# Five norms of an encoder in a different order, a softmax multiply moved to DVE, a last norm read from its bank

## The chip, the core and the metric

The kernel runs on one core of a Trainium2 chip. The metric is device time in microseconds (us), the median of several runs. The core's engines are named as in the profile: PE multiplies matrices, DVE and ACT work along rows of 128 partitions, POOL is the third of that kind, and SP issues transfers. Each engine works through its own queue in order and waits at semaphores for what other engines or transfers have to finish first.

## The reference, cut

Two requests of 512 and 256 tokens go through the same two layers, one of each kind, with a model width of 1024. The kernel lays them side by side as 768 columns.

```python
def rmsnorm(x, g, eps=NORM_EPS):
    return x * lax.rsqrt(jnp.mean(x * x, axis=-1, keepdims=True) + eps) * g

for layer in range(DEPTH):                       # 2
    if layer % 2 == 0:
        h = rmsnorm(x, ln_mix_e[j])
        qa, ka, va, qb, kb, vb = jnp.split(h @ w_in_e[j], EVEN_SPLITS, axis=-1)
        a_out = neighbourhood_attention(qa, ka, va, rpb[j])
        qb, kb = rope(rmsnorm(qb, q_norm_b[j])), rope(rmsnorm(kb, k_norm_b[j]))
        b_out = gqa_attention(qb, kb, vb)        # 8 query heads on 2 key heads, softmax
        x = x + jnp.concatenate([a_out, b_out], axis=-1) @ w_out_e[j]
    else:
        h = rmsnorm(x, ln_mix_o[j])
        qc, kc, vc = jnp.split(h @ w_in_o[j], ODD_SPLITS, axis=-1)
        o = rmsnorm(diff_attention(rope(qc), rope(kc), vc, lam), subln_g[j]) * (1.0 - lam_init)
        x = x + o.reshape(B, T, DIFF_WIDTH) @ w_out_o[j]
    h = rmsnorm(x, ln_mlp[layer])
    x = x + jnp.square(jax.nn.relu(h @ w_up[layer])) @ w_down[layer]
return rmsnorm(x, ln_f)
```

## The kernel before

**Layout.** Everything is kept feature by token: x is eight tiles of 128 features by 768 tokens, six token tiles of 128 (TT). Each 32-bit operand of a projection is split into a high part, made by a copy (whi, xh), and a low part, the remainder (wlo, xl), and a product is three matmuls: high by high, high by low, low by high. Functions wsplit (L76) and split (L108) make the parts; the high one is ACT's (or DVE's for every other weight piece at the start), the low one DVE's.

**A norm (class Norm, L127).** The rows of x carry the gain only; the factor 1/rms of each token is applied behind the projection. add (L140) squares a feature tile on ACT and adds it to acc on DVE. rstd (L154) sums acc over the features by tiny matmuls into ss (L161), scales it to ms on DVE (L164) and raises it to the power -1/2 on POOL, rt (L166), one column for each token tile. Where a factor along the columns is needed, spread (L169) makes it by matmuls into the bank pb (L178) and DVE copies that to R (L180). PSUM has eight banks in two groups, three named mm and five named at; a tile waits until the readers of an earlier tile in its bank are done.

**Stages in order.** even_attention (L303) loads x and the first weights, splits them in a loop over eight feature tiles (L320) with the squares of the tile before in each turn, projects keys and values of the six token tiles (proj_kv, tile kvp; kv_out scales them by rt and hands the keys to norm_rope) and then the queries (proj_q, tile qp). Its tables function calls rstd and builds the rotary tables. Attention units and further projections alternate. A unit of the query heads takes two heads: scores gs, their maximum m (DVE, L495), ge = exp (ACT, L497), reciprocal ri (DVE, L500), and the division of both heads' ge, one on DVE (L501), one on POOL (L502); six units for each pair of heads, 24 in all, of 512 keys or of 256. Then ge is transposed on PE (gpt_ps, L443) and multiplied by the values. The odd layer projects values first (proj_v, tile dvp, ACT's dv behind it) and then queries and keys (dqk). Each MLP is a product in seven partial products (up, L856, and dn, L1022) on sums c of quarters of x (t and c at L792 to L817); finish (L869) multiplies the result z by R. The last norm (final, L1065) runs in two halves of 384 tokens: squares, rstd, spread, and eight multiplies by gain and R (L1093), each followed by its transfer out, alternately on SP's and on ACT's queue.

**What sets the order.** A scheduler places the instructions of each engine's queue by the order in which the code is written, by priorities (tc.high_priority() raises them) and by estimated readiness. On the chip each queue is fixed.

Of the kernel before, what the change touches and what calls it, by code (L numbers as in the profile page):

```python
# [37 lines left out]
def kernel(ctx: ExitStack, tc: tile.TileContext, a: dict, y: bass.AP):  # L38
# [22 lines left out]
    def ps_tile(tag, name):  # L61
        return psum.tile([P, 512], F32, tag=tag, name=name, bufs=BANKS[tag])
# [66 lines left out]
    def gcol(g, k):  # L129
        return gains[:, g, k : k + 1]  # L130

    class Norm:
# [22 lines left out]
        def rstd(self, s0=0):  # L155

            n = len(self.tiles)
            ss = ps_tile("at", "ss")
            for i, t in enumerate(self.tiles):
                for j, part in enumerate(self.parts):  # L160
                    nc.tensor.matmul(ss[:, 2 * i : 2 * i + 2], part[:, t * P - s0 : (t + 1) * P - s0], ones,  # L161
                                     start=j == 0, stop=j == len(self.parts) - 1)
            ms = spool.tile([P, TT], F32, tag="ms", name="ms", bufs=2)[:, :n]
            nc.vector.tensor_scalar(ms, ss[:, 0 : 2 * n : 2], 1.0 / D, 1e-6, op0=ALU.mult, op1=ALU.add)  # L164
            rt = cpool.tile([P, TT], F32, tag="rt", name="rt", bufs=2)[:, :n]
            nc.gpsimd.tensor_tensor(out=rt, in0=ms, in1=nhalf[:, :n], op=ALU.pow)  # L166
            return rt

        def spread(self, rt, R=None):  # L169

            if R is None:
                R = cpool.tile([P, NT], F32, tag="R", name="R", bufs=1)
            for c in range(0, len(self.tiles), 4):
                ts_ = self.tiles[c : c + 4]
                s, e = ts_[0] * P, ts_[-1] * P + P
                pb = ps_tile("at", "pb")
                for i, t in enumerate(ts_):
                    nc.tensor.matmul(pb[:, i * P : (i + 1) * P], rt[:, c + i : c + i + 1].broadcast_to([P, P]), ident,  # L178
                                     start=True, stop=True)
                nc.vector.tensor_copy(R[:, s:e], pb[:, : e - s])  # L180
            return R


    def proj_tok(col, xs, t, ps):
# [116 lines left out]
    def even_attention():  # L301
# [18 lines left out]
        for k in range(KD):  # L320
            c = slice((k % 4) * 256, (k % 4) * 256 + 256)
            wsplit(w0[k // 4][0][:, c], w0[k // 4][1][:, c], raws[k // 4][:, c], k % 2 == 0)
            xs.append(split(x0s[k], "x", gcol(G_E, k)))
            if k:
                nm.add(x0s[k - 1])
        nm.add(x0s[KD - 1])
        col0 = wcol(w0)

        ropeE = xo_tile("ropeE").rearrange("p (a t d) -> p a t d", a=2, d=HD)
# [64 lines left out]
        def proj_kv():  # L394
            col = col0
            kT.append(qk("gk"))

            gv.append(ap.tile([P, 9, P], F32R, tag="v", name="gv", bufs=3)[:, :8, :].rearrange("p (t a) (b d) -> p t (a b) d", a=2, b=2))
            gv.append(ap.tile([P, 2, 4, HD], F32R, tag="gvp", name="gvp", bufs=1))
            pend = []  # L400
            for t in range(TT):
                ps = ps_tile("mm" if t < 3 else "at", "kvp")
                yield from proj_tok(col, xs, t, ps)
                pend.append((t, ps))
                if t == 3:
                    tables()
                while pend and t >= 3:
                    kv_out(*pend.pop(0))

        def kv_out(t, ps):  # L410
            r = rts[0][:, t : t + 1]
            v = gv[t // 4][:, t % 4]
            pv = ps[:, P:256].rearrange("p (h d) -> p h d", d=HD)
            nc.scalar.activation(v[:, 0:4:3], pv, AF.Copy, scale=r)
            nc.vector.scalar_tensor_tensor(out=v[:, 1:3], in0=pv, scalar=r, in1=v[:, 0:4:3].bitcast(F32),
                                           op0=ALU.mult, op1=ALU.subtract)
            norm_rope(ps[:, :P], 2, t, tabs[1], kT)

        def proj_q(s):
            col = wgroup("w_in_e")  # L420
            for j in range(2):
                gq[2 * s + j] = qk(f"gq{2 * s + j}")
            for t in range(TT):
                ps = ps_tile("mm", "qp")
                yield from proj_tok(col, xs, t, ps)
                norm_rope(ps[:, :256], 4, t, tabs[0], [gq[2 * s], gq[2 * s + 1]])

# [48 lines left out]
        def gqa_unit(j, t):  # L476
            if t == 0:
                o[j] = xo_tile("go")
            if t % 2 == 0:
                vals.append(Values(j, t))  # L480
                del vals[:-2]
            now = vals[-1]
            prev = vals[-2] if len(vals) > 1 else None
            q, k = gq[j], kT[0]
            tk = slice(t * P, (t + 1) * P)
            k0, nk = (0, 4) if t < 4 else (TS, 2)
            ks = slice(k0, k0 + nk * P)
            l2 = spool.tile([P, 2], F32, tag="l2", name="l2")

            def f_s():  # L490
                ss = scores("gs", nk * P, lambda i, hp, s: q[hp, i, s], lambda i, hp, s: k[hp, i, s], tk, ks)
                es_ = []
                for h, s in enumerate(ss):
                    m = spool.tile([P, 1], F32, tag="m", name="m")
                    nc.vector.tensor_reduce(out=m, in_=s, axis=AX.X, op=ALU.max, negate=True)  # L495
                    e = ap.tile([P, 512], F32, tag="e", name="ge", bufs=6)[:, : nk * P]
                    nc.scalar.activation(e, s, AF.Exp, bias=m, scale=1.0, accum_out=l2[:, h : h + 1])  # L497
                    es_.append(e)
                ri = spool.tile([P, 2], F32, tag="ri", name="ri")
                nc.vector.reciprocal(ri, l2)  # L500
                nc.vector.tensor_scalar(es_[0], es_[0], ri[:, 0:1], None, op0=ALU.mult)  # L501
                nc.gpsimd.tensor_tensor(out=es_[1], in0=es_[1], in1=ri[:, 1:2].broadcast_to([P, nk * P]), op=ALU.mult)  # L502
                now.es.append(es_)

            def f_t():
                v = now if t % 2 else prev
                if v:
                    v.turn()

            def f_v():  # L510
                v = now if t % 2 else prev
                if v:
                    v.values()

            return f_s, f_t, f_v, lambda: None


# [98 lines left out]
    def odd_attention(xs, nm, sg, spill):  # L616
# [17 lines left out]
        def proj_v(n):  # L634
            col = wgroup("w_in_o")
            v = vs[n] = ap.tile([P, TT, 256], F32, tag="v", name=f"dv{n}", bufs=2)
            pend = []
            for t in range(TT):
                ps = ps_tile("mm" if n or t < 3 else "at", "dvp")
                yield from proj_tok(col, xs, t, ps)  # L640
                pend.append((t, ps))
                if not rts and t == TT - 1:
                    rts.append(nm.rstd())
                while rts and pend:
                    t_, ps = pend.pop(0)
                    nc.scalar.activation(v[:, t_, :], ps[:, :256], AF.Copy, scale=rts[0][:, t_ : t_ + 1])  # L646
# [419 lines left out]
    def final(x, sq, s):  # L1066

        acc = cpool.tile([P, NT], F32, tag="acc", name="acc", bufs=1) if s else accs[0]
        R = cpool.tile([P, NT], F32, tag="R", name="R", bufs=1) if s else accs[1]
        accs[:] = [acc, R]  # L1070
        ms = (0, 2, 4, 6, 1, 3, 5, 7) if s else (1, 3, 5, 7, 0, 2, 4, 6)
        sl = slice(s, s + HT)
        nm = Norm(None, (s, s + HT), acc)
        rt = []

        def part(i):
            if i == 0:
                nc.scalar.activation(acc[:, sl], x[ms[0]][:, sl], AF.Square)
                nm.parts = [acc[:, sl]]
                for n, m in enumerate(ms[1:]):  # L1080
                    t = sq()
                    nc.scalar.activation(t, x[m][:, sl], AF.Square)
                    if n < 5:
                        nc.vector.tensor_tensor(out=acc[:, sl], in0=acc[:, sl], in1=t, op=ALU.add)
                    else:
                        nm.parts.append(t)
            elif i == 1:
                rt.append(nm.rstd(s))
            else:
                nm.spread(rt[0], R)  # L1090
                for k in ms:
                    yt = x[k][:, sl]
                    nc.vector.scalar_tensor_tensor(out=yt, in0=yt, scalar=gcol(G_F, k), in1=R[:, sl], op0=ALU.mult, op1=ALU.mult)  # L1093
                    (nc.sync, nc.scalar)[k // 2 % 2].dma_start(y[:, k, sl], yt)

        return part
# [146 lines left out]
```

## Time and profile before

| | us |
|---|---|
| median of three runs | 1766.36 (1765.38 to 1767.30) |
| the profiled execution, its own time | 1770.48 |
| its span in the trace | 1768.2 |
| PE busy | 1721.2 (97%) |
| DVE busy | 1396.3 (79%) |
| ACT busy | 825.0 (47%) |
| POOL busy | 593.0 (34%) |

The span runs from the first to the last recorded instruction; the rest of the execution's own time lies around it. The mean granted clock of PE over the span is 0.987 of full speed. A line of the waits says which tile an engine waited for, who released it, and for how long. A line of the timeline has the start, the length, the engine, the line of the kernel, and the tile with its sources; behind it in brackets the idle time of the engine before it and what ended that. [...]

### The profile page before, as it was taken

The page shows a single profiled execution, that of the slowest core. Times are in us where ns is not written, and L with a number is a line of the kernel's source. Part 1 is how long each engine was busy: PE and PEld are TensorE (multiplying, and loading weights), DVE is VectorE, ACT ScalarE, POOL GpSimd, SP SyncE. Part 2 cuts the span into 40 slices and gives each one's busy share as a digit, 9 for nine tenths or more (in the row PEclk, how much of TensorE's full clock was granted, in tenths as well). Part 3 has the DMA queues.
Part 4 walks back from the last instruction along what each step waited for, and adds up shares of the span by engine and source line. Part 5 has one row for each costly group of instructions (what it writes and reads, how often), then busy time and mean ns, then how long its engine had stood idle before and what let it go on. Part 6 is the DMA issues. An engine that isn't in the chain of part 4 may idle for free.

```text
span 1768.2 us, 28354 instructions
## 1 busy us (share of the span) xinstructions
PE 1721.2 (97%) x10994; PEld 1635.5 (92%) x10994; DVE 1396.3 (79%) x2182; ACT 825.0 (47%) x1509; POOL 593.0 (34%) x456
## 2 busy tenths in 40 slices
PE   7999999999999999999999999999989999999997
PEld 7887888899999999999999999988989999999997
DVE  7777746588899878799656767776898888797995
ACT  6675544354333354444425555554543333544441
POOL 1421000023555505475021212220236556054750
PEclk8999999999999999999999999999999999999998
DMA  4111223312554497764211101112124544977621
GB/s 167 49 34 37 69 67 101 125 55 99 166 165 166 165 342 280 285 199 158 97 48 49 45 29 46 51 55 94 57 99 165 166 157 162 338 290 268 220 90 72
DMA packets 74597, 235.42 MB, mean 133 GB/s; under 512 B 7904, under 2 KB 25056, under 8 KB 74464
## 3 DMA queue, kind: packets, MB, share of 16 engines
q1 hardware_dynamic: 52480, 186.93, 31.7%
q0 software_dynamic: 7168, 25.17, 3.8%
q10 hardware_dynamic: 14816, 21.52, 3.4%
q8 instruction: 86, 1.41, 0.3%
q14 instruction: 47, 0.39, 0.1%
HBM read 182.47 MB, written 50.33 MB: 132 GB/s over the span
## 4 chain that ended last, share of the span: by engine, by line
PE 67%; DVE 18%; issue 7%; ACT 4%; POOL 2%; DMA 1%; DVEq 0%; POOLq 0%; SPq 0%; ACTq 0%
PE dn L1022 25%; PE dqk L190 8%; PE up L856 6%; PE opa L202 5%; PE dvp L190 4%; DVE z L875 3%; DVE wlo L81 3%; DVE z L864 3%; PE opb L202 3%; PE npa L202 2%; DVE t L864 2%; PE ds L268 2%; PE dpv L716 2%; ACT z L877 2%; DVE t L792 2%
## 5 line engine op out<-in xcount | busy, mean ns | idle before, releaser
L856 PE MATMUL up<-c,whi 128*128 128x384 f32 x1824 | 469.8, 339 | 0.0
L1022 PE MATMUL dn<-th,whi 128*128 128x384 f32 x1792 | 460.8, 338 | 0.0
L856 PEld LDWEIGHTS up<-c,whi 128*128 128x128 f32 x1824 | 332.6, 189 | 0.1
L1022 PEld LDWEIGHTS dn<-th,whi 128*128 128x128 f32 x1792 | 325.7, 188 | 0.7 <-DVE th L117 0.5
L856 PE MATMUL up<-c,wlo 128*128 128x384 f32 x912 | 310.1, 340 | 3.8 <-DVE wlo L81 3.6
L1022 PE MATMUL dn<-th,wlo 128*128 128x384 f32 x896 | 302.9, 338 | 0.5 <-DVE wlo L81 0.5
L986 POOL TENSOR_TENSOR ch<-ch,wd 128x1024 f32<-128x1024 f32 x60 | 187.6, 3136 | 117.7 <-DVE wlo L81 94.5
L841 POOL TENSOR_TENSOR s<-wraw 128x512 f32<-128x512 f32 x56 | 105.8, 1907 | 331.6 <-DMA wraw<-in_w_up_dram 308.0
L81 DVE TENSOR_TENSOR wlo<-ch,whi 128x1024 fp32r<-128x1024 f32 x88 | 166.9, 1912 | 27.7 <-ACT whi L80 27.4
L856 PEld LDWEIGHTS up<-c,wlo 128*128 128x128 f32 x912 | 172.3, 189 | 8.5 <-DVE wlo L81 8.3
L80 ACT ACTIVATE whi<-ch 128x1024 fp32r<-128x1024 f32 x88 | 93.2, 1064 | 176.6 <-PE dn L1022 138.8
L1022 PEld LDWEIGHTS dn<-th,wlo 128*128 128x128 f32 x896 | 168.2, 188 | 1.1 <-DVE wlo L81 1.1
L117 DVE TENSOR_TENSOR th<-tr,th 128x1536 fp32r<-128x1536 f32 x56 | 142.8, 2553 | 12.8 <-ACT th L116 12.7
L81 DVE TENSOR_TENSOR wlo<-wraw,whi 128x1024 fp32r<-128x1024 f32 (+3 forms) x132 | 136.3, 1034 | 17.5 <-ACT whi L80 17.0
L80 ACT ACTIVATE whi<-wraw 128x1024 fp32r<-128x1024 f32 (+3 forms) x128 | 116.8, 914 | 68.0 <-PE opb L202 24.6
L190 PE MATMUL dqk<-whi,xh 128*128 128x256 f32 x384 | 116.1, 302 | 2.2 <-ACT dv L646 2.2
L877 ACT ACTIVATE z<-z 128x1536 f32<-128x1536 f32 x32 | 47.7, 1489 | 140.5 <-DVE z L875 139.5
L190 PE MATMUL dqk<-whi,xl 128*128 128x256 f32 x384 | 108.6, 283 | 0.0
L190 PE MATMUL dqk<-wlo,xh 128*128 128x256 f32 x384 | 108.4, 282 | 0.0
L701 ACT ACTIVATE de<-ds,m 128x512 f32<-128x512 f32 (+1 forms) x96 | 58.4, 613 | 81.7 <-DVE m L699 81.7
L116 ACT ACTIVATE th<-tr 128x1536 fp32r<-128x1536 f32 x56 | 82.8, 1478 | 24.4 <-DMA tr<-T 15.6
L864 DVE TENSOR_TENSOR z<-up,z 128x384 f32<-128x384 f32 x168 | 89.8, 548 | 4.5 <-PE up L856 4.4
(217 smaller groups left out, 3772.6 us busy)
## 6 DMA issues: line engine op xcount, KB each, us to landing
wd<-in_w_down_dram SPq DMA_DIRECT2D x84, 512.0 KB, 4.9
tr<-T SPq DMA_DIRECT2D x56, 768.0 KB, 5.3
wraw<-in_w_up_dram SPq DMA_DIRECT2D x64, 512.0 KB, 3.7
T<-t POOLq DMA_DIRECT2D x64, 384.0 KB, 3.0
T<-z ACTq DMA_DIRECT2D x32, 576.0 KB, 3.0
ch<-in_w_down_dram SPq DMA_DIRECT2D x28, 512.0 KB, 7.4
wraw<-in_w_in_o_dram SPq DMA_DIRECT2D x24, 512.0 KB, 3.7
wraw<-in_w_in_e_dram SPq DMA_DIRECT2D x16, 512.0 KB, 3.8
```

What stands on the lines that cost most here:

```text
L80: nc.scalar.activation(hi, raw, AF.Copy)
L81: nc.vector.tensor_tensor(out=lo, in0=raw, in1=hi.bitcast(F32), op=ALU.subtract)
L116: nc.scalar.activation(hi, src, AF.Copy)
L117: nc.vector.tensor_tensor(out=lo, in0=src, in1=hi.bitcast(F32), op=ALU.subtract)
L190: nc.tensor.matmul(ps[:, :256], st[:, tk], col(k, part, 0, 256), start=(k == 0 and i == 0), stop=(k == KD - 1 and i == 2))
L202: nc.tensor.matmul(ps[:, : e - s], w, mv[:, s:e], start=(k == 0 and i == 0), stop=(k == nk - 1 and i == 2))
L841: nc.gpsimd.tensor_tensor(out=d_, in0=x_, in1=y_, op=ALU.add)
L856: nc.tensor.matmul(ps, part[a_][:, base + k * P : base + (k + 1) * P], t[:, b_], start=start and k + i == 0, stop=stop and k == 3 and i == 2)
L864: nc.vector.tensor_tensor(out=out, in0=x_, in1=y_, op=op)
L877: nc.scalar.activation(z, z, AF.Square)
L986: nc.gpsimd.tensor_tensor(out=t, in0=t, in1=new.pop((i, rp)), op=ALU.add)
L1022: nc.tensor.matmul(ps, w[a_][:, c : c + P], th[:, b_, q], start=i + q + a_ + b_ == 0, stop=i == NG - 1 and q == ND - 1 and a_ == 1)
```

## The change

It has six parts.

1. In rstd, ms and rt are placed at high priority, in every norm.
2. In the first norm, the squares come behind all eight splits, and rstd and all uses of rt come behind the sixth token tile of keys and values instead of the fourth. The first query tile takes its bank from the at group.
3. In the odd layer rstd is called behind the fourth value tile instead of the sixth.
4. In the query heads' softmax the second head's ge is divided by DVE as well.
5. spread is cut in two; bcast makes the bank pb alone. In the last norm the multiplies of DVE read R from that bank and not from a copy.
6. In the second half of the last norm (s = 0), three feature tiles are multiplied by the gain beforehand on ACT, R is copied from the bank by ACT, and POOL multiplies these three by R; DVE has the other five. One more tile of squares is added to acc there, so ss has two parts instead of three.

```diff
@@ rstd
-            nc.vector.tensor_scalar(ms, ss[:, 0 : 2 * n : 2], 1.0 / D, 1e-6, op0=ALU.mult, op1=ALU.add)
             rt = cpool.tile([P, TT], F32, tag="rt", name="rt", bufs=2)[:, :n]
-            nc.gpsimd.tensor_tensor(out=rt, in0=ms, in1=nhalf[:, :n], op=ALU.pow)
+            with tc.high_priority():
+                nc.vector.tensor_scalar(ms, ss[:, 0 : 2 * n : 2], 1.0 / D, 1e-6, op0=ALU.mult, op1=ALU.add)
+                nc.gpsimd.tensor_tensor(out=rt, in0=ms, in1=nhalf[:, :n], op=ALU.pow)
@@ even_attention, splits
-            if k:
-                nm.add(x0s[k - 1])
-        nm.add(x0s[KD - 1])
+        for x0 in x0s:
+            nm.add(x0)
@@ proj_kv
-                if t == 3:
+                if t == TT - 1:
                     tables()
-                while pend and t >= 3:
-                    kv_out(*pend.pop(0))
+                    while pend:
+                        kv_out(*pend.pop(0))
@@ proj_q
-                ps = ps_tile("mm", "qp")
+                ps = ps_tile("mm" if s + t else "at", "qp")
@@ gqa_unit
                 nc.vector.tensor_scalar(es_[0], es_[0], ri[:, 0:1], None, op0=ALU.mult)
-                nc.gpsimd.tensor_tensor(out=es_[1], in0=es_[1], in1=ri[:, 1:2].broadcast_to([P, nk * P]), op=ALU.mult)
+                nc.vector.tensor_scalar(es_[1], es_[1], ri[:, 1:2], None, op0=ALU.mult)
@@ odd layer, proj_v
-                if not rts and t == TT - 1:
+                if not rts and t == 3:
                     rts.append(nm.rstd())
@@ final
-                    if n < 5:
+                    if n < (5 if s else 6):
...
+                if not s:
+                    for k in ms[:3]:
+                        nc.scalar.activation(x[k][:, sl], x[k][:, sl], AF.Copy, scale=gcol(G_F, k))
...
-                nm.spread(rt[0], R)
+                early = () if s else ms[:3]
+                pb = nm.bcast(rt[0])
+                if early:
+                    nc.scalar.activation(R[:, sl], pb, AF.Copy)
                 for k in ms:
                     yt = x[k][:, sl]
-                    nc.vector.scalar_tensor_tensor(out=yt, in0=yt, scalar=gcol(G_F, k), in1=R[:, sl], op0=ALU.mult, op1=ALU.mult)
+                    if k in early:
+                        nc.gpsimd.tensor_tensor(out=yt, in0=yt, in1=R[:, sl], op=ALU.mult)
+                    else:
+                        nc.vector.scalar_tensor_tensor(out=yt, in0=yt, scalar=gcol(G_F, k), in1=pb, op0=ALU.mult, op1=ALU.mult)
```

Line numbers behind the first part move by up to 15. Three places of the instruction order follow.

**PE at the start**, around the sums of the first norm (ss); kvp are the keys and values, qp the queries. Before:

```order
L190 MATMUL kvp<-whi,xh 128x256
L190 MATMUL kvp<-wlo,xh 128x256
L190 MATMUL kvp<-whi,xl 128x256 x4
L161 MATMUL ss<-ones,acc 128x2 x6
L190 MATMUL kvp<-whi,xh 128x256
```

Now:

```order
L196 MATMUL kvp<-whi,xh 128x256
L196 MATMUL kvp<-wlo,xh 128x256
L196 MATMUL kvp<-whi,xl 128x256
L161 MATMUL ss<-ones,acc 128x2 x6
L196 MATMUL qp<-whi,xh 128x256
L196 MATMUL qp<-wlo,xh 128x256
```

Before, 96 kvp matmuls stand ahead of ss and 48 behind it; now all 144 stand ahead, and two query tiles of 24 matmuls each follow.

**DVE at the first MLP's norm**; t and c are the sums of quarters of x, wlo a weight's low part. Before:

```order
L792 SCALAR_TENSOR_TENSOR t<-x_4166,gains,t 128x384 x3
L117 TENSOR_TENSOR c_4752<-t,c_4752 128x384
L81 TENSOR_TENSOR wlo<-wraw,whi 128x512
L117 TENSOR_TENSOR c_4756<-t,c_4756 128x384
L117 TENSOR_TENSOR c_4760<-t,c_4760 128x384
L117 TENSOR_TENSOR c_4763<-t,c_4763 128x384
L792 SCALAR_TENSOR_TENSOR t<-x_4250,gains,t 128x384
L164 TENSOR_SCALAR ms<-ss 128x6
L792 SCALAR_TENSOR_TENSOR t<-x_4319,gains,t 128x384 x3
L117 TENSOR_TENSOR c_4770<-t,c_4770 128x384
```

Now:

```order
L797 SCALAR_TENSOR_TENSOR t<-x_4082,gains,t 128x384
L797 SCALAR_TENSOR_TENSOR t<-x_4166,gains,t 128x384 x3
L166 TENSOR_SCALAR ms<-ss 128x6
L81 TENSOR_TENSOR wlo<-wraw,whi 128x512
L117 TENSOR_TENSOR c_4752<-t,c_4752 128x384
L117 TENSOR_TENSOR c_4756<-t,c_4756 128x384
L117 TENSOR_TENSOR c_4760<-t,c_4760 128x384
L117 TENSOR_TENSOR c_4763<-t,c_4763 128x384
L797 SCALAR_TENSOR_TENSOR t<-x_4250,gains,t 128x384
L797 SCALAR_TENSOR_TENSOR t<-x_4319,gains,t 128x384 x3
```

ms, with POOL's rt behind it, stands ahead of one wlo, the four c and one t that it stood behind.

**PE in the odd layer's value projection**, around ss. Before:

```order
L190 MATMUL dvp_8984<-wlo_8855,xh_8784 128x256
L190 MATMUL dvp_8984<-whi_8854,xl_8785 128x256
L161 MATMUL ss_9009<-ones_77,acc_8764 128x2 x6
L190 MATMUL dqk_9040<-whi_9028,xh_8791 128x256
L190 MATMUL dqk_9040<-wlo_9029,xh_8791 128x256
L190 MATMUL dqk_9040<-whi_9028,xl_8792 128x256
```

Now:

```order
L196 MATMUL dvp_8934<-wlo_8855,xh_8784 128x256
L196 MATMUL dvp_8934<-whi_8854,xl_8785 128x256
L161 MATMUL ss_8959<-ones_77,acc_8764 128x2 x6
L196 MATMUL dvp_8974<-whi_8848,xh_8791 128x256
L196 MATMUL dvp_8974<-wlo_8849,xh_8791 128x256
L196 MATMUL dvp_8974<-whi_8848,xl_8792 128x256
```

ss has moved ahead of the last two value tiles; before, the first query and key tile dqk followed it at once.

## Rows read from the trace of the kernel before

**Rows 1.** Waits of PE: tile and line, releaser, us in total, times, longest
```profile
PE pb L178 <- POOL rt L166: 9.9, 3, 5.0
...
PE kvp L190 <- ACT xh L119: 5.5, 1, 5.5
...
PE gpt_ps L443 <- DVE ge L501: 4.2, 4, 2.2
...
PE dqk L190 <- ACT dv L646: 2.2, 1, 2.2
```

**Rows 2.** Windows: us, busy (count) of PE, PEld, DVE, ACT, POOL; clock, DMA
```profile
22.00:45.00 23.00, 19.12 (x117) 18.34 (x117) 16.48 (x60) 10.03 (x32) 7.98 (x13) 0.78 0.24 68
65.00:193.00 128.00, 120.07 (x838) 101.17 (x838) 100.82 (x213) 80.23 (x217) 30.49 (x35) 0.99 0.11 32
415.00:420.00 5.00, 5.00 (x21) 5.00 (x20) 4.78 (x7) 1.24 (x2) 0.00 (x0) 0.50 0.00 0
535.00:640.00 105.00, 102.73 (x577) 99.86 (x576) 95.14 (x109) 41.95 (x44) 49.43 (x35) 1.00 0.60 206
```

**Rows 3.** Timeline of the start: begin, length, row, [idle before it, releaser]
```profile
20.21 1.01 DVE L120 SCALAR_TENSOR_TENSOR xl<-x,gains,xh 128x768 fp32r<-128x768 f32 x1
...
21.14 0.95 DVE L152 TENSOR_TENSOR acc<-acc,sq 128x768 f32<-128x768 f32 x1
...
23.48 2.17 PE L161 MATMUL ss<-ones,acc 128*128 128x2 f32 x12 [1.46 <-DVE acc L152]
...
26.01 1.51 POOL L166 TENSOR_TENSOR rt<-ms,nhalf 128x6 f32<-128x6 f32 x1 [24.69 <-DVE ms L164]
...
27.56 1.14 ACT L414 ACTIVATE gv<-kvp,rt 128x128 fp32r<-128x128 f32 x4 [6.87 <-POOL rt L166]
```

**Rows 4.** Timeline of the first query-head softmaxes, DVE and POOL
```profile
65.38 0.48 DVE L501 TENSOR_SCALAR ge<-ge,ri 128x512 f32<-128x512 f32 x1
...
69.57 1.04 POOL L502 TENSOR_TENSOR ge<-ge,ri 128x512 f32<-128x512 f32 x1 [2.48 <-DVE ss L354]
...
69.67 1.22 DVE L501 TENSOR_SCALAR ge<-ge,ri 128x512 f32<-128x512 f32 x1
```

**Rows 5.** Groups by line and shape, DVE: busy us, mean ns, idle before
```profile
L501 DVE TENSOR_SCALAR ge<-ge,ri 128x512 f32<-128x512 f32 x16 | 14.3, 893 | 0.6
```

**Rows 6.** Timeline of the first MLP's norm, DVE, POOL and PE
```profile
406.80 2.31 DVE L792 SCALAR_TENSOR_TENSOR t<-x,gains,t 128x384 f32<-128x384 f32 x4
...
412.27 1.69 POOL L166 TENSOR_TENSOR rt<-ms,nhalf 128x6 f32<-128x6 f32 x1 [8.22 <-DVE ms L164]
...
414.02 2.93 PE L178 MATMUL pb<-ident,rt 128*128 128x128 f32 x12 [3.76 <-POOL rt L166]
...
422.50 0.96 DVE L864 TENSOR_TENSOR t<-z 128x768 f32<-128x768 f32 x1 [1.00 <-ACT z L877]
...
426.86 0.56 DVE L864 TENSOR_TENSOR z<-up,z 128x384 f32<-128x384 f32 x1 [2.21 <-PE up L856]
```

**Rows 7.** Timeline of the second MLP's norm, PE
```profile
1301.38 2.93 PE L178 MATMUL pb<-ident,rt 128*128 128x128 f32 x12 [4.96 <-POOL rt L166]
```

**Rows 8.** Timeline of the odd layer's norm, PE and POOL
```profile
881.66 0.28 PE L190 MATMUL dvp<-whi,xl 128*128 128x256 f32 x1
...
881.78 1.40 PE L161 MATMUL ss<-ones,acc 128*128 128x2 f32 x12
...
883.46 1.34 POOL L166 TENSOR_TENSOR rt<-ms,nhalf 128x6 f32<-128x6 f32 x1 [60.07 <-DVE ms L164]
...
885.75 0.42 PE L190 MATMUL dqk<-wlo,xh 128*128 128x256 f32 x1
...
885.96 0.41 PE L190 MATMUL dqk<-whi,xl 128*128 128x256 f32 x1
```

**Rows 9.** Timeline of the last norm's second half, DVE
```profile
1754.59 0.55 DVE L864 TENSOR_TENSOR x<-x,dn 128x384 f32<-128x384 f32 x1 [0.93 <-PE dn L1022]
...
1760.94 4.32 DVE L1093 SCALAR_TENSOR_TENSOR x<-x,gains,R 128x384 f32<-128x384 f32 x8
```

More of the change, by code (lines that the diff above doesn't have):

```diff
@@ L173, in spread, with bcast @@
             for c in range(0, len(self.tiles), 4):
[L174 to L180, printed above, removed]
-            return R
+                pb = self.bcast(rt, c)
+                s = self.tiles[c] * P
+                nc.vector.tensor_copy(R[:, s : s + pb.shape[1]], pb)
+            return R
+        def bcast(self, rt, c=0):
+            ts_ = self.tiles[c : c + 4]
+            pb = ps_tile("at", "pb")
+            for i in range(len(ts_)):
+                nc.tensor.matmul(pb[:, i * P : (i + 1) * P], rt[:, c + i : c + i + 1].broadcast_to([P, P]), ident,
+                                 start=True, stop=True)
+            return pb[:, : len(ts_) * P]
     def proj_tok(col, xs, t, ps):
```

## The prediction

> **What bounds the kernel now.** I read the page's busy times first: PE is busy for 97% of the span, DVE for 79%. Little can come from shorter work on the other engines; only PE's remaining idle time and its clock can be won. So the second view is PE's waits, [rows 1]. The longest there by releaser is pb behind POOL's rt, 9.9 us in three waits, the chain ss, ms, rt, pb of a norm; then gpt_ps behind DVE's softmax multiply, 4.2, and dqk behind ACT's dv, 2.2, which hangs on a norm's rt too. [...] After the 3.76 us idle of the first MLP [rows 6] the granted clock is 0.50 from 415 to 420 [rows 2]. [...] Last, what stands behind PE: in the up stage both engines are tight, PE 102.7 and DVE 95.1 us of 105 [rows 2], and PE waits for weights that DVE splits, so a lead of PE alone is not kept there.
>
> **Start (squares behind all splits).** Before, the first 96 kvp matmuls end at 22.0 (ss begins at 23.48 after 1.46 idle [rows 3]). From 22 to 45 PE is busy for 19.1 of 23 us at a mean clock of 0.78 [rows 2]: 3.9 us idle and 23 x 0.22 = 5.1 us of clock, 9.0 lost together. After, all 144 kvp matmuls come before ss. They start at 5.5 as now [rows 1] and take 16.8 us at 0.117, so 22.4 at the earliest; with no use of PE's present gaps 27.6. The last xl ends at 21.2, and two accumulations of 0.95 [rows 3] that stood ahead of it now stand behind it: 19.3. About 35 matmuls (4.1 us) then remain, and I take 24.4, 3.2 ahead of the 27.6. The rest of DVE's accumulations end by 23.1, in time for ss. A new wait appears: ss to 25.8, ms, rt 1.5 us to about 27.6 (POOL is alone), six ACT copies at 0.29 [rows 3] and the squares that free the banks, so that a bank for the second query tile is free at about 30.7. PE fills that with the 24 matmuls of the first query tile, to 28.7, and waits 2.0 us, with 2.6 of slow clock behind it. DVE's later weight split costs another 1.0. Gain 3.2 + 9.0 - 2.0 - 2.6 - 1.0 = **6.6**, from 4.0 (a second such wait) to 9.2 (the clock holds). ms and rt at high priority move nothing here: DVE splits one weight half ahead of ms, which ends before ss does.
>
> **First MLP norm.** ms moves from behind a row of t to right behind the four t that end at 409.1 [rows 6], so rt ends near 411.0 and pb starts 3.0 earlier. PE's idle shrinks from 3.76 to 0.8; at the higher level pb takes a little over half of its 2.93, some 1.7 (1.3 less), and the up matmuls behind it run at half rate from 416.6 to about 419.5, which costs 1.4: 5.7 on PE. DVE does the same rows in the same order otherwise. It can move ahead only by its idle time before the loop settles, 1.00 and 2.21 [rows 6], 3.2 us, and PE needs DVE's weights from then on. I take **3.4**, from 1.0 to 5.7. No queue but DVE's is moved past: the t and c rows behind ms come 0.15 us later, which PE reads only three products (6 us) on.
>
> **Odd layer.** The ss matmuls stand behind four dvp tiles instead of six. Two tiles, 48 x 0.117 = 5.6 us, cover ms, the 1.3 us of rt and dv; POOL has been idle for 60 us there [rows 8] and DVE is done with the accumulations. ss itself costs the same. The 2.2 wait goes and with it 2.5 of clock: **4.7**, from 4.0 to 5.0, next in line is dqk's own weight, whose hi part ACT now makes behind five dv copies; PE needs it only after the two tiles.
>
> **Second MLP norm.** The same with a longer wait, 4.96 [rows 7]; ms passes four more rows. PE: 4.2 + 1.3 + 1.4 = 6.9. DVE's two idle times behind it are there too, about as long. I take **3.6**, from 1.0 to 6.9.
>
> **Query-head softmax.** 24 multiplies go from POOL to DVE. DVE's own takes 0.48 us alone; at the longest wait it took 1.22, beside a POOL multiply of 1.04, and ended 0.3 after it [rows 4]. The mean is 0.89 [rows 5]. With both on DVE two in a row take 0.97: 0.25 sooner than the 1.22, and hardly more of DVE than now (16 x 0.08 = 1.3 us for the wide units, as much again for the eight narrow ones, on 100.8 of 128 [rows 2]). At most the gain is the 4.2 of waits and a slow stretch of about 1.5, since the changed order also puts more projection matmuls of PE ahead of the first transposes; at worst POOL's remaining rn rows and that order (weight splits and reductions move on DVE) cost 2. I take **2.5**, between -2.0 and 5.7.
> [...]
>
> **Last norm.** Before, a copy of R and eight multiplies of 0.54 [rows 9] end 4.9 us after pb. After, an ACT copy (0.5) and five multiplies on DVE, since the copy and DVE read the bank in turn: 3.2; POOL's three at 3/4 of 1.04 to 1.22 [rows 4] give 2.8 to 3.3, and two transfers on SP's queue stand behind POOL's third. Six ss records fewer give 0.4. I take **0.3**, from -0.9 to 1.4. A PSUM operand costs nothing extra: the same shape with one took 0.55 [rows 9].
> [...]
>
> **Sum.** 6.6 + 3.4 + 4.7 + 3.6 + 2.5 + 0.3 = 21.1. The profiled execution took 1770.48 us, 4.1 above the median of the runs, so it would be 1749.4; the median 1766.36 becomes **1745.3**.
>
> **The rivals.** First: DVE follows PE in both MLPs, because its rows there wait for PE's results, and the clock survives the new wait of the start. That adds 2.3 + 3.3 + 2.6 = 8.2: 1737. For it: DVE's present waits on PE in these loops; against it: PE's own waits for wlo. Second: the early ms is used up. DVE's next rows come no earlier, ACT's z and the split weights end the wait instead, the first two waits of the start repeat themselves: MLPs 1.0 each, start 4.0, softmax 1.0, the odd layer and tail as summed: 12.0, so 1754.4. For it: DVE is busy for 4.78 of the 5 us in which PE works at the lower level [rows 2]. Third, slower: in the head stage DVE becomes the bound. If each second multiply is held up as the 1.22 us row was, 24 x (1.22 - 0.48) = 17.8 us come on top on DVE, and where PE waits for them, three more waits of 2.2 with slow stretches of 1.5 bring 11.1: in place of the gain of 2.5 a loss of 28.9, 1776.7. It decides once the loss passes 18.6. Against it: DVE has 27 us of idle time there. Fourth: the priority has no effect, ms stays late in both MLPs, as if unchanged: 1745.3 + 7.0 = 1752.3; but the order of DVE's queue shows ms moved, so this is nearly excluded.
>
> **How the numbers follow.** Forecast 0.50 (own range 1740 to 1750), first rival 0.18, second 0.25, third 0.04, fourth and others 0.03. The 8-in-10 range reaches into the first two: 1736 to 1757. What a measurement can tell from no change is 0.2%, 3.5 us. Faster takes all but the third rival and a remainder: 0.94; same 0.03; slower 0.03.
>
> **What would show it.** Right: no wait of pb above 1.0 in the MLPs, dqk without a wait, 144 kvp before ss, one wait of qp behind kv_out, a clock near 1.0 at 415 to 420 and 885 to 890, no gpt_ps wait of 2 us. Wrong: up waits for wlo or c summing to the 5.7 and 6.9 that pb gave; qkT and qp waits at the start as before; DVE multiplies of 1 us with POOL's rn beside them; a last multiply later than 4.9 us after pb. The largest doubt is the start, whose new wait I have timed from sums alone.

## The result

The changed kernel takes **1744.15 us** (median of four runs, 1741.66 to 1745.31), the kernel before 1766.83 beside it. The ratio is 0.9867, with a 95% interval of 0.9848 to 0.9886: 23.5 us faster, 20 to 27. The forecast was 1745.3, in a range of 1736 to 1757.

The two profiled executions differ by more, 1770.48 to 1743.15 us, in span 1768.2 to 1741.4. Of these 27.3 us, 3.7 come from the execution of before, which lies that far above its median, and 1.0 from the changed one, which lies below its own. One of the four executions of e11 below, 2773.86 us at a mean granted clock of 0.556, is left out of its ratio.

### The profile page after: what moved, and what is told of

It is laid out like the page before. It is cut to its first block, busy times and chain, and to the rows that moved or that the text cites. A ratio compares the mean times of both kernels' runs of the same rounds, so it can differ in the third digit from the quotient of the medians.

```text
span 1741.4 us, 28288 instructions
## 1 busy us (share of the span) xinstructions
PE 1710.9 (98%) x10988; PEld 1622.0 (93%) x10988; DVE 1396.1 (80%) x2202; ACT 823.5 (47%) x1513; POOL 571.3 (33%) x435
## 4 chain that ended last, share of the span: by engine, by line
PE 69%; DVE 19%; issue 6%; ACT 4%; POOL 1%; DMA 1%; POOLq 0%; DVEq 0%; ACTq 0%; SPq 0%
PE dn L1027 26%; PE dqk L196 8%; PE opa L208 5%; DVE z L880 4%; PE dvp L196 4%; DVE z L869 3%; DVE wlo L81 3%; PE npa L208 3%; PE opb L208 3%; DVE t L869 3%; DVE t L797 2%; ACT z L882 2%; PE ds L274 2%; PE dpv L721 2%; PE qp L196 2%
## 5 line engine op out<-in xcount | busy, mean ns | idle before, releaser
L861 PEld LDWEIGHTS up<-c,wlo 128*128 128x128 f32 x912 | 171.3, 188 | 12.4 <-DVE wlo L81 12.1
```

The source lines that it names most:

```text
L861: nc.tensor.matmul(ps, part[a_][:, base + k * P : base + (k + 1) * P], t[:, b_], start=start and k + i == 0, stop=stop and k == 3 and i == 2)
```

## The profile after

PE's waits in the changed kernel, in the columns of [rows 1]:

```profile
PE kvp L196 <- ACT xh L119: 5.5, 1, 5.5
...
PE up L861 <- DVE wlo L81: 4.7, 15, 0.5
...
PE qp L196 <- DVE work L369: 2.5, 1, 2.5
...
PE pb L185 <- POOL rt L167: 2.5, 3, 1.2
...
PE up L861 <- ACT z L911: 1.3, 1, 1.3
```

pb's 9.9 us are 2.5, gpt_ps behind ge and dqk behind dv are gone from the list. New is one wait of qp at the start, 2.5 us, and up waits somewhat more than before.

Windows of the changed kernel, in the columns of [rows 2]; the stretches answer to 22 to 45, 65 to 193 and 415 to 420 there, the second row is the one that holds the new wait. A row begins with the stretch and its length; the clock is a share of full speed, and the two figures behind it are the share and the GB/s of the transfers. Read in slices of 0.5 us, the clock of before from 22 to 45 us is 1.00 or 0.50 in all but four, in which it changes; these two are called its higher and its lower level here.

```profile
22.00:45.00 23.00, 20.46 (x173) 20.10 (x173) 19.98 (x82) 14.17 (x48) 11.59 (x20) 1.00 0.16 47
30.00:35.00 5.00, 3.25 (x27) 3.28 (x28) 4.25 (x26) 4.36 (x14) 2.71 (x7) 1.00 0.22 80
65.00:193.00 128.00, 127.32 (x879) 107.47 (x878) 103.78 (x242) 79.88 (x213) 5.39 (x8) 1.00 0.13 41
402.00:407.00 5.00, 5.00 (x30) 5.00 (x29) 4.77 (x6) 1.74 (x4) 0.00 (x0) 1.00 0.00 0
```

PE is busy for 20.5 of 23 us in the first (19.1 before) and the clock is 1.00 instead of 0.78. From 65 to 193 us, in the heads' stage, PE stands still for 0.7 us where it was 7.9; the changed kernel is some 11 us further on in its work there, and from 53.7 to 181.7 it is 0.7 us too. Behind the first MLP's norm the clock is 1.00 where it was 0.50, and not only in the row shown: it is 1.00 from the first matmul of pb on.

Timeline of the start, PE, DVE, POOL and ACT, answering to [rows 3]:

```profile
24.87 1.40 PE L161 MATMUL ss<-ones,acc 128*128 128x2 f32 x12
...
26.38 1.23 DVE L81 TENSOR_TENSOR wlo<-wraw,whi 128x1024 fp32r<-128x1024 f32 x1
...
26.62 2.19 POOL L167 TENSOR_TENSOR rt<-ms,nhalf 128x6 f32<-128x6 f32 x1 [25.30 <-DVE ms L166]
...
28.85 1.14 ACT L419 ACTIVATE gv<-kvp,rt 128x128 fp32r<-128x128 f32 x4 [4.12 <-POOL rt L167]
...
31.75 0.36 PE L196 MATMUL qp<-whi,xh 128*128 128x256 f32 x1 [2.54 <-DVE work L369]
```

ss begins at 24.87 without a wait, all 144 kvp matmuls ahead of it. rt took 2.19 us here against 1.51 before; the row above it shows DVE at a weight split that began ahead of rt and lay beside it for 1.0 us. PE then does the 24 matmuls of the first query tile and waits 2.54 us for the bank of the second.

Timeline of the first MLP's norm, answering to [rows 6]:

```profile
395.59 0.15 DVE L166 TENSOR_SCALAR ms<-ss 128x6 f32<-128x6 f32 x1
...
395.82 1.78 POOL L167 TENSOR_TENSOR rt<-ms,nhalf 128x6 f32<-128x6 f32 x1 [5.21 <-DVE ms L166]
...
397.66 1.60 PE L185 MATMUL pb<-ident,rt 128*128 128x128 f32 x12 [0.60 <-POOL rt L167]
...
408.14 0.95 DVE L869 TENSOR_TENSOR t<-z 128x768 f32<-128x768 f32 x1
...
410.20 0.55 DVE L869 TENSOR_TENSOR z<-up,z 128x384 f32<-128x384 f32 x1
```

ms stands 0.2 us ahead of rt, pb starts after 0.60 us of idle time and takes 1.60 for its 12 matmuls (2.93 before). The last two rows are those of DVE that had idled for 1.00 and 2.21; neither has an idle time now.

The odd layer's norm, answering to [rows 8]:

```profile
858.62 1.39 PE L161 MATMUL ss<-ones,acc 128*128 128x2 f32 x12
...
865.56 0.28 PE L196 MATMUL dqk<-whi,xh 128*128 128x256 f32 x1
```

ss ends at 860.0, two value tiles follow, and dqk starts without a wait.

The last norm's second half, answering to [rows 9]:

```profile
1733.40 0.49 ACT L1102 ACTIVATE R<-pb 128x384 f32<-128x384 f32 x1 [4.20 <-PE pb L185]
...
1733.92 2.71 DVE L1108 SCALAR_TENSOR_TENSOR x<-x,gains,pb 128x384 f32<-128x384 f32 x5 [3.19 <-ACT R L1102]
...
1733.97 2.90 POOL L1106 TENSOR_TENSOR x<-x,R 128x384 f32<-128x384 f32 x3 [2.31 <-ACT R L1102]
```

DVE's five multiplies read R from the bank and take 2.71 us, 0.54 each, as they did from the copy [rows 9]. The first begins 0.03 us behind the end of ACT's copy from the same bank, which released it. POOL's three end 0.2 us after them.

## Experiments

Seven kernels take one part of the change alone or undo one; three more change what stands behind a part. Apart from the medians each gives stages by the start of the same matmuls: from the start to ss of the first MLP's norm, from there to the first value projection of the odd layer (dvp), on to ss of the second MLP, and to the last dn.

| kernel | ratio to before | ss, MLP 1 | to dvp | to ss, MLP 2 | to last dn |
|---|---|---|---|---|---|
| before | | 400.3 | 464.7 | 421.5 | 467.7 |
| changed | 0.9867 (0.9848 to 0.9886) | 387.1 | 460.3 | 416.3 | 464.0 |
| e1, part 2 alone | 0.9957 (0.9942 to 0.9972) | 393.8 | 464.7 | 419.6 | 467.2 |
| e2, part 4 alone | 0.9960 (0.9945 to 0.9975) | 393.8 | 462.4 | 421.8 | 467.0 |
| e3, part 1 alone | 0.9975 (0.9965 to 0.9985) | 400.4 | 462.1 | 418.5 | 464.6 |
| e4, part 3 alone | 0.9979 (0.9970 to 0.9989) | 397.4 | 465.5 | 416.7 | 467.1 |
| e5, parts 5 and 6 alone | one run | 400.6 | 463.5 | 420.5 | 467.5 |
| e6, changed without part 4 | 0.9905 (0.9889 to 0.9922) | 390.1 | 461.4 | 415.8 | 464.7 |
| e7, changed without part 2 | 0.9908 (0.9892 to 0.9925) | 395.9 | 459.9 | 415.8 | 463.7 |

### e1: the start alone

```diff
-            if k:
-                nm.add(x0s[k - 1])
-        nm.add(x0s[KD - 1])
+        for x0 in x0s:
+            nm.add(x0)
...
-                if t == 3:
+                if t == TT - 1:
                     tables()
...
-                ps = ps_tile("mm", "qp")
+                ps = ps_tile("mm" if s + t else "at", "qp")
```

> Part 2 of the change alone (first norm's squares behind the splits, all six key and value tiles ahead of ss, first query tile's bank from the other group), in the kernel before. The trace of the changed kernel has the first MLP's ss 13.2 us earlier than before (387.1 against 400.3), where the prediction gave start and softmax 6.6 + 2.5 = 9.1; its clock is 1.00 from 20 to 40 us although PE waits 2.54 us there. Theory: the start alone gives about 9 (the clock holds), so ss of the first MLP stands at about 391 and the median is near 1758. Rival: the start gives 6.6 or less and the clock falls after its new wait as it fell after the others; ss near 394, median near 1760.

Measured: ratio 0.9957, 7.6 us (4.9 to 10.2); ss of the first MLP at 393.8. Timeline of PE in e1, the new wait and, from the odd layer, dqk with its unchanged wait:

```profile
32.36 0.55 PE L190 MATMUL qp<-whi,xh 128*128 128x256 f32 x1 [2.54 <-DVE work L363]
...
878.89 0.58 PE L190 MATMUL dqk<-whi,xh 128*128 128x256 f32 x1 [2.19 <-ACT dv L645]
...
879.49 0.41 PE L190 MATMUL dqk<-whi,xl 128*128 128x256 f32 x1
...
879.70 0.41 PE L190 MATMUL dqk<-whi,xh 128*128 128x256 f32 x1
```

The window of e1 with the new wait:

```profile
30.00:35.00 5.00, 2.64 (x12) 2.67 (x13) 4.25 (x24) 4.36 (x15) 2.59 (x6) 0.71 0.29 93
```

The wait is the changed kernel's, 2.54 us, but here the granted clock fell behind it (0.71; 1.00 in the changed kernel in the same stretch). So neither is right as it stands: the clock falls after this wait in one execution and not in another. The trace is the rival's in every point (the clock fell, ss at 393.8); it is that of the slowest of e1's four executions, 1762.23 us. The median gain, 7.6, lies between the rival's 6.6 and the theory's 9.

### e2: the softmax alone

```diff
-                nc.gpsimd.tensor_tensor(out=es_[1], in0=es_[1], in1=ri[:, 1:2].broadcast_to([P, nk * P]), op=ALU.mult)
+                nc.vector.tensor_scalar(es_[1], es_[1], ri[:, 1:2], None, op0=ALU.mult)
```

> Part 4 alone (both heads' softmax multiplies on DVE), in the kernel before. Theory: the four waits of gpt_ps for DVE go (4.2 us) and the slow stretch behind the longest, a gain of 3 to 5 us at the first MLP's ss, with DVE's multiplies at 0.49 us each. Rival: its gain in the changed kernel came from the start, which reordered PE's queue there; alone it gives under 1.5 us, and a wait of about 2 us for DVE stays.

Measured: ratio 0.9960, 7.1 us (4.4 to 9.7), more than either expected in the median; ss of the first MLP stands 5.9 us ahead of the mean, 399.7 (that of before, e3, e4 and e5, whose code is the same up to there and whose values go from 397.4 to 400.6). The place of [rows 4] in e2, DVE and PE:

```profile
68.11 0.48 DVE L501 TENSOR_SCALAR ge<-ge,ri 128x512 f32<-128x512 f32 x1
...
68.50 0.48 DVE L502 TENSOR_SCALAR ge<-ge,ri 128x512 f32<-128x512 f32 x1
...
68.64 0.87 PE L443 MATMUL gpt_ps<-ident,ge 128*128 128x128 f32 x6 [0.29 <-DVE ge L501]
```

And the group of [rows 5], with the second head's beside it:

```profile
L501 DVE TENSOR_SCALAR ge<-ge,ri 128x512 f32<-128x512 f32 x16 | 7.7, 484 | 0.3
...
L502 DVE TENSOR_SCALAR ge<-ge,ri 128x512 f32<-128x512 f32 x16 | 7.7, 480 | 0.0
```

The first head's multiply takes 0.484 us in the mean of its 16 rows. The 0.89 of before was a mean of two kinds: eight multiplies of 0.48 to 0.49 us, and eight of 1.22 to 1.36, beside a multiply of POOL that had begun before them or at most 0.04 us behind. Where POOL's began 0.11 us or more behind, DVE's was not held. The transposes start when that one is done, at 68.64, while the second still runs: they do not wait for two in a row.

### e3: the priority alone

```diff
-            nc.vector.tensor_scalar(ms, ss[:, 0 : 2 * n : 2], 1.0 / D, 1e-6, op0=ALU.mult, op1=ALU.add)
...
-            nc.gpsimd.tensor_tensor(out=rt, in0=ms, in1=nhalf[:, :n], op=ALU.pow)
+            with tc.high_priority():
+                nc.vector.tensor_scalar(ms, ss[:, 0 : 2 * n : 2], 1.0 / D, 1e-6, op0=ALU.mult, op1=ALU.add)
+                nc.gpsimd.tensor_tensor(out=rt, in0=ms, in1=nhalf[:, :n], op=ALU.pow)
```

> Part 1 alone (ms and rt at high priority), in the kernel before. Theory: the waits of pb in both MLPs fall below 1 us and the up stages end 4.3 and 3.7 us earlier, as between the two traces, 8 together, median near 1759: the first loop passes keep part of PE's 5.7 and 6.9, DVE sets the rest. Rival 1: PE's whole gain is kept, 12.6 us, near 1754. Rival 2: the gain is taken up by waits of up, 2 us, near 1765.

Measured: ratio 0.9975, 4.4 us (2.6 to 6.2). The two norms' pb in e3, and dqk between them, whose wait is as before:

```profile
411.23 1.60 PE L179 MATMUL pb<-ident,rt 128*128 128x128 f32 x12 [0.88 <-POOL rt L167]
...
882.90 0.39 PE L191 MATMUL dqk<-whi,xh 128*128 128x256 f32 x1 [2.19 <-ACT dv L647]
...
883.24 0.28 PE L191 MATMUL dqk<-whi,xl 128*128 128x256 f32 x1
...
883.36 0.28 PE L191 MATMUL dqk<-whi,xh 128*128 128x256 f32 x1
...
1291.62 1.60 PE L179 MATMUL pb<-ident,rt 128*128 128x128 f32 x12 [0.66 <-POOL rt L167]
```

PE's waits for the up stages, in the kernel before and, below it, in e3:

```profile
PE up L856 <- DVE wlo L81: 3.6, 10, 0.5
...
PE up L857 <- DVE wlo L81: 6.0, 17, 0.6
...
PE up L857 <- ACT z L907: 1.3, 1, 1.3
```

pb behaves as in the changed kernel, but the up stages give part of it back: up's waits for wlo grow from 3.6 to 6.0 us and one for ACT's z is new. Over all kernels of the table and e10 and e11 below, the stage from ss to dvp takes 463.5 us without part 1 (460.5 to 465.5) and 460.9 with it (459.9 to 462.1), from the second ss to the last dn 467.0 and 464.2: 2.6 and 2.8 us. Rival 2's 2 us and the theory's 8 both miss; this is well short of what PE gains from ss to the end of pb, 4.1 and 5.5 us in the same means, and by the higher clock behind it. The first of these stages varies by 5 us without any change to it, so its 2.6 is less certain than the second's 2.8.

### e4: the odd layer alone

```diff
-                if not rts and t == TT - 1:
+                if not rts and t == 3:
```

> Part 3 alone (odd layer's rstd behind the fourth value tile), in the kernel before. Theory: dqk starts without a wait and at the higher clock; the second MLP's ss stands 4.7 to 5.2 us earlier, all else as before, median near 1762. Rival: a later wait in the layer takes the gain, under 2 us. Its start and heads are those of the kernel before, so its trace also tells how far their waits differ from one execution to another.

Measured: ratio 0.9979, 3.7 us (1.9 to 5.3). The stage that holds the edit takes 416.7 us; in the six kernels with this part it is 415.8 to 416.7, in the others 418.5 to 421.8, so 4.3 less in the mean. The theory's mechanism holds; the gain is somewhat below its 4.7 to 5.2. What was not expected stands in the first column: ss of the first MLP comes 2.9 us earlier than in the kernel before, with the same code up to there. Windows of three kernels whose start is the same as before; e3:

```profile
25.00:30.00 5.00, 5.00 (x24) 5.00 (x25) 3.11 (x14) 1.92 (x7) 2.02 (x2) 0.50 0.01 2
35.00:40.00 5.00, 2.94 (x14) 2.59 (x14) 5.00 (x19) 2.77 (x12) 3.82 (x6) 0.80 0.25 63
```

e4:

```profile
25.00:30.00 5.00, 5.00 (x32) 5.00 (x32) 3.31 (x15) 2.28 (x8) 2.21 (x2) 0.69 0.01 2
35.00:40.00 5.00, 4.10 (x33) 3.91 (x34) 5.00 (x15) 2.17 (x9) 2.43 (x4) 1.00 0.46 129
```

e5:

```profile
25.00:30.00 5.00, 5.00 (x31) 5.00 (x32) 3.67 (x18) 2.37 (x9) 2.53 (x4) 0.68 0.01 2
35.00:40.00 5.00, 4.29 (x20) 4.04 (x20) 3.87 (x12) 1.47 (x5) 2.31 (x3) 0.51 0.55 134
```

The waits there are the same in all of them (1.47 us ahead of ss, 1.0 ahead of qkT, 0.7 to 0.8 ahead of qp), but the clock behind them is 0.50, 0.68 or 0.69, and 0.51, 0.80 or 1.00.

### e5: the last norm alone

```diff
-                    if n < 5:
+                    if n < (5 if s else 6):
...
+                    if k in early:
+                        nc.gpsimd.tensor_tensor(out=yt, in0=yt, in1=R[:, sl], op=ALU.mult)
```

The other lines of parts 5 and 6 go with it.

> Parts 5 and 6 alone (last norm read from the bank, POOL and ACT helping in its second half), in the kernel before. Theory: from the last dn matmul to the end of the span 0 to 1 us less than before, as forecast (0.3); nothing else moves. Rival: POOL's three multiplies hold SP's transfers, the end comes later, by up to 0.9 us. Its first 300 us are those of the kernel before, so it also gives another sample of the granted clock after the unchanged waits of the start (so far 0.50 to 0.69 in 25 to 30 us and 0.66 to 1.00 in 35 to 40).

Measured: one run, 1767.77 us beside 1768.19. From the last dn to the end 13.7 us against 14.0, and 13.7 in the changed kernel. Over all traces this stretch is 13.3 to 14.6 without the two parts and 13.2 to 14.0 with them. So 0.3 is in line with the forecast, but less than the stretch varies by itself, and a gain is not shown.

### e6 and e7: one part undone

```diff
 e6, from the changed kernel
-                nc.vector.tensor_scalar(es_[1], es_[1], ri[:, 1:2], None, op0=ALU.mult)
+                nc.gpsimd.tensor_tensor(out=es_[1], in0=es_[1], in1=ri[:, 1:2].broadcast_to([P, nk * P]), op=ALU.mult)
 e7, from the changed kernel
-        for x0 in x0s:
-            nm.add(x0)
+            if k:
+                nm.add(x0s[k - 1])
...
-                if t == TT - 1:
+                if t == 3:
```

> The changed kernel with part 4 undone (second head's multiply back on POOL). Part 4 alone gave 7.1 us in the median (ratio 0.996). Theory: it acts by itself, through DVE's own multiply, which took 0.89 us in the mean beside POOL's and 0.48 without it; undone, the changed kernel is 4 to 7 us slower, about 1750, and gpt_ps waits for DVE again. Rival: with the new start PE has enough projection work queued in the heads' stage to hide it, under 2 us.

> The changed kernel with part 2 undone (squares among the splits, ss behind four key and value tiles, as before). Theory: the start acts by itself; ss of the first MLP stands 6 to 9 us later than in the changed kernel (387.1), at about 394, and the median is near 1751 to 1753. The traces so far (start alone 393.9 and 390.2, without it 397.4 to 400.6) differ by 3 us among themselves with the granted clock of 25 to 40 us. Rival: the heads' stage gives the time back, under 3 us.

Measured: 1750.74 us (ratio 0.9905) and 1750.61 (0.9908); against the changed kernel's 0.9867 that is 0.38% and 0.41%, 6.7 and 7.2 us, the same as each alone (7.1 and 7.6). In e6 gpt_ps waits for DVE's multiply again, 2.0 us in three; the wait of 2.2 that before had is not among them. e6's trace, of the fastest of its four executions (1747.39 us), has ss of the first MLP only 3.0 us behind the changed kernel's; in e7 it is 8.8 behind, as its theory had it. By the medians the two parts act by themselves, and both rivals fall.

### e11: the second multiply on ACT

```diff
-                nc.gpsimd.tensor_tensor(out=es_[1], in0=es_[1], in1=ri[:, 1:2].broadcast_to([P, nk * P]), op=ALU.mult)
+                nc.scalar.activation(es_[1], es_[1], AF.Copy, scale=ri[:, 1:2])
```

> The kernel before with the second head's multiply on ACT instead of POOL: it takes away POOL's work beside DVE as part 4 does, but puts none on DVE. Theory: what part 4 gains is DVE's own multiply and the rows behind it, no longer held by POOL; then this gains as much as part 4, 5 to 8 us, with DVE's multiply at 0.48. Rival: POOL's multiply itself was late for the transposes; then ACT's longer queue (80 us busy of 128, 24 rows of some 0.6 more) gives less, under 3 us.

Measured: ratio 0.9944 (0.9927 to 0.9961), 9.9 us (6.9 to 12.9); ss of the first MLP at 393.4. The window of the heads' stage in e11:

```profile
65.00:193.00 128.00, 124.12 (x870) 105.33 (x869) 96.61 (x224) 95.37 (x247) 6.64 (x10) 0.99 0.12 33
```

DVE's multiply there:

```profile
L501 DVE TENSOR_SCALAR ge<-ge,ri 128x512 f32<-128x512 f32 x16 | 7.7, 483 | 0.3
```

DVE's multiply takes 0.48 us again, DVE has 7 us less to do than in e2, and the gain is no smaller than e2's (the intervals overlap). So part 4 gains by taking the second multiply off POOL; no price shows for DVE's doing twice as many. Both kernels also relieve POOL's queue. That the gain comes through DVE's multiply and not through POOL's own being late is borne out by PE's waits before: those of the transposes name DVE's ge, 4.2 us, and never POOL's.

In e2, with POOL's other rows still there, both multiplies take 0.48 us in the mean: no row of POOL's shows as holding the second one.

### e8: the copies of R on ACT

```diff
-                nc.vector.tensor_copy(R[:, s : s + pb.shape[1]], pb)
+                nc.scalar.activation(R[:, s : s + pb.shape[1]], pb, AF.Copy)
```

> The changed kernel with the MLP norms' two copies of R made by ACT instead of DVE (ACT stands idle there). It takes 1.0 us off DVE's queue ahead of each up loop, and nothing off PE's. Theory: DVE sets where the up loops end, so each ends about 1 us earlier, 2 in all, near 1742. Rival: PE sets it, the part of its gain that is missing (5.7 and 6.9 forecast, 2.7 and 3.1 seen with part 1 alone) went elsewhere, and this gives nothing.

Measured: 1742.98 us, ratio 0.9857 (0.9842 to 0.9872). The edit also moves a third copy, in the heads' stage. The intervals overlap with the changed kernel's, so this does not show a faster version. In the trace the stage to dvp takes 459.6 us and the last one 463.6, 1.3 and 0.7 below the means with part 1. That is the way the theory has it, but less than these stages vary (459.9 to 462.1 and 463.7 to 464.7): whether DVE or PE sets the loops' end stays open.

### e10: a longer wait at the start

```diff
-            nc.scalar.activation(v[:, 0:4:3], pv, AF.Copy, scale=r)
+            for _ in range(9 if t == 0 else 1):
+                nc.scalar.activation(v[:, 0:4:3], pv, AF.Copy, scale=r)
```

> The changed kernel with ACT's first copy of the values (gv of token tile 0) done nine times instead of once, 8 x 0.29 = 2.3 us longer ahead of the copies that free the banks. In the changed kernel PE waits 2.5 us there, after 24 matmuls without a gap, and the clock stayed at 1.00 in three of four traces of this start. Theory: what decides is how long PE has stood; with a wait of 4.8 us the granted clock falls, as after the 3.8 and 4.8 us of pb in every trace, and the first MLP's ss stands about 2.3 + 2.6 = 5 us later, at 392. Rival: the place decides, the clock holds, and ss stands 2.3 later or less, at 389.

Measured: one run, 1748.83 us. The new wait in e10:

```profile
36.61 0.55 PE L196 MATMUL qp<-whi,xh 128*128 128x256 f32 x1 [6.84 <-DVE work L369]
```

The window around its end:

```profile
35.00:40.00 5.00, 3.39 (x16) 3.42 (x17) 4.57 (x30) 3.78 (x13) 3.40 (x9) 0.50 0.40 117
```

The wait came out at 6.8 us and not 4.8, since ACT's other copies were put in another order too. The clock is 0.50 behind it, and ss of the first MLP stands at 391.9, 4.7 later than in the changed kernel. That this is near the theory's 5 is chance, as the wait alone grew by 4.3. The place does not keep the clock up, as e1 showed too. That a longer wait loses it each time is not shown by one trace.

## Why the prediction was right

The time and the direction hold, and no term has the wrong sign. Measured by medians, the parts alone add up to 7.6 + 7.1 + 4.4 + 3.7 = 22.8 us and the tail's few tenths, against 21.1 in the sum and 23.5 measured. The single sizes are off in both directions, softmax 4.6 above its term, the MLPs 2.6 below theirs. That the sum came out within 1.2 us of the measured time is luck: these errors cancel. The mechanisms held, but for the comparison in the softmax term and the 24.4 of the start, both below.

**Start: 6.6 forecast, 7.6 alone, 7.2 undone.** The steps hold to half a us up to ms: kvp done at 24.4 (24.87), ms at 25.8 (26.3). rt then ended 1.2 us later than summed (28.8 for 27.6), with 2.19 us beside DVE's weight split, and the bank came free 1.0 later (31.75 for 30.7); as PE was later too, the wait is 2.54 for 2.0. The 24.4 itself was partly luck: 19.3 and 4.1 make 23.4, the 1.0 on top had no reason given, and the 22.4 at the earliest prices all 144 matmuls at 0.117. In the changed kernel no wait is left among them, and the first 22, behind the 5.5 us of the start, stand 0.21 us apart and more, the lower level; that makes the 24.87. The term for the clock behind the new wait, 2.6, is a chance: it was paid in e1 and not in the changed kernel, e6 and e8. By traces the start gives 5.9 us where it was paid (e1, against the mean 399.7) and 8.8 where it was not (changed kernel against e7), where the sum had 6.6 and 9.2.
The same power took 1.34 in the odd layer with no DVE row at its side (860.29 in the changed kernel); that the split is what lengthened it is inferred from the two, and no run isolates it.

**Softmax: 2.5 forecast, 7.1 alone, 6.7 undone.** This is the term that was mis-sized most. The step that failed is the comparison of two multiplies in a row, 0.97, with the 1.22 of one: 0.25 sooner. The first transposes wait for the first head alone, so 1.22 to 1.36 become 0.48 in eight of the 16 wide units, 0.74 to 0.88 sooner each. gpt_ps's waits for ge went from 4.2 to 0.7 us in e2, those of gs behind ACT's ge from 1.7 to 0.8; that the latter comes from DVE's maxima moving up too is argued and not shown. The traces put the term lower than the medians: from the first scores (gs) to the first MLP's ss it is 340.5 to 341.3 us in before, e3, e4 and e5, and 335.2 to 335.6 in e2, e7 and e11, some 5 us.

**The MLPs: 3.4 + 3.6 forecast, 4.4 alone.** PE gains at pb what the sum said (ss to the end of pb: 16.6 us before, 12.1 after, and the clock behind it). DVE's two idle times went, as said. Of that the stages keep 2.6 and 2.8 us, somewhat below the 3.4 and 3.6. From the end of pb on they take 1.5 and 2.7 us longer with part 1 than without it, though the slow stretch there is gone. More waits of up are a part of that: for wlo and z they are 6.5 us in the mean of the kernels with part 1 and 2.9 without; where the rest goes stays open. The prediction took DVE's 3.2 of idle time as what can be kept. The size fits, but no run isolates it. The first rival, that PE's whole gain is kept, is out; the second, 1.0 each, misses the stages' 2.6 and 2.8 as well.

**Odd layer: 4.7 forecast, 3.7 alone, 4.3 in the stage.** The wait and its slow stretch went. The term's 2.5 of clock is what before's trace shows: 26 dqk matmuls behind the wait, from 885.37 to 890.87, stand 0.21 us apart and more, those ahead of it 0.117 (the first of each in [rows 8]), some 0.096 us more each. The stretch was overrated: in e1 it followed the wait at once (matmuls 0.21 us apart), in e3, with the same wait of 2.19, it did not (0.12).

**Last norm: 0.3 forecast, 0.3 in e5, within what the stretch varies.** The bank costs DVE nothing, 0.54 us a multiply. POOL's three took 2.90, in the forecast's 2.8 to 3.3, though the 1.22 of [rows 4] in that term is a DVE row and not one of POOL's.

**The base.** The rows were read in an execution 4.1 us above the median, at a mean granted clock of 0.987, where the other executions of the kernel have 0.988 to 0.991. In the trace the excess is spread: some 1 us in each of the table's four stages, above the mean of the kernels that leave that stage alone. Slow stretches of it were booked as fixed costs, and a part of them is what the change removes. The medians therefore differ by 23 us and not by the traces' 27. That the clock makes up this excess fits its means, but it is not taken apart here.

**The slower side**, DVE as the bound of the heads' stage, did not come: DVE is busy for 103.8 of 128 us there.

## What to carry to other kernels

Where two engines share one softmax, look at which half the next engine needs first, and price the multiply that it waits for and not the pair. Do not expect to keep the whole of a wait taken off the leading engine in front of a loop in which a second engine is nearly as busy: here some half of PE's gain was kept, close to the idle time that the second engine had left, though that this set it is not shown. A mean can hide two kinds: half of the multiplies behind the 0.89 were not held at all. Look at several executions before a slow-clock stretch is booked as a fixed cost.

## What the runs showed of the hardware

The granted clock behind the same wait differs between executions of the same code: 0.50 to 0.69 in 25 to 30 us and 0.51 to 1.00 in 35 to 40 behind the unchanged start, 0.71 or 1.00 in 30 to 35 behind a wait of 2.54 us, and behind dqk's 2.2 us it fell at once in before and e1 (matmuls 0.21 us apart) and not at all in e3 (0.12), and behind 3.1 us in e11 a few matmuls later. After 3.5 to 5 us ahead of the MLPs' pb it was at the lower level at least for part of the following matmuls in every trace without part 1 (12 matmuls of pb took 1.91 to 2.93 us, and in e5's first MLP seven took 1.87), after 6.8 ahead of qp in e10 too (0.50), and after 0.6 to 0.9 ahead of pb in no trace with part 1 (12 in 1.60). The length alone does not decide in these runs: behind 1.2 us ahead of the last norm's pb the clock was 0.50 in before and in the changed kernel (six matmuls in 1.65 us, as in e5; 1.18 in e8), behind 1.3 ahead of up (the wait for z) it was low in none of six (1.00 in the changed kernel, and from the third matmul on 0.17 to 0.18 us apart in all six).

A POOL power of 128x6 took 1.34 us in the changed kernel's odd layer with no DVE row beside it, and 2.19 when a DVE subtraction with both inputs in SBUF was already under way as it began. In before's odd layer such a subtraction began 0.2 us behind it, and the power took 1.34 again. In e2 and e11 dqk waited 3.1 us instead of 2.2 in the odd layer, 0.9 more, about what 2.19 is above 1.34; the power's own length there is not shown.
